# Issuing every second load of expert weights from ScalarE's queue instead of SyncE's

## The chip, the cores and the metric

The kernel runs on one core of a Trainium2 chip. A core has a matrix engine (TensorE, in the profile PE and PEld for its weight loads), VectorE (DVE), ScalarE (ACT), GpSimd (POOL) and SyncE (SP), each with one instruction stream that it works off in order, and DMA engines that move data between the chip's memory (HBM) and the core's own (SBUF). A transfer is issued by an instruction in the stream of some engine; an issue waits in that stream until the buffer that it fills is free. The metric is device time in microseconds (us).

## The reference

One sequence of 256 tokens with 1024 features goes through three blocks. All values are float32.

- Block 0: normalisation, a mixer of two linear recurrences (a gated one and retention), and a feed-forward layer with squared ReLU of 4096 features.
- Block 1: the same with a gated matrix memory (mLSTM) as mixer.
- Block 2: normalisation with a learnt shift and scale, causal attention of 8 heads beside a gated convolution, and a mixture of experts.

The mixture of experts is the part that matters here. A router scores 4 groups of 8 experts for each token; the token takes the best group and the two best experts in it. Each expert is a small network, and its result is weighted by the router:

```
g_idx = argmax(g_logits)
e_val, e_loc = top_k(e_logits[g_idx], 2)
hid = silu(xb @ w1[e]) * (xb @ w3[e])      # 1024 -> 512
y   = hid @ w2[e]                          # 512 -> 1024
out[tok] += weight * y
```

With 32 experts, `w1`, `w3` and `w2` are 201 MB, and the kernel reads all of it, whatever the router says.

## The kernel before, in words

The kernel is one Python function that traces instructions; a scheduler then puts each engine's instructions into one stream. It goes by an estimate of when an instruction can start, and among those that are ready by the order in which they were traced; `keep_in_program_order` pins an instruction behind the one traced before it on its engine. The stream is fixed before the program runs.

Up to the router the work is dense products. A weight unit of 1 MB (128 partitions x 4 x 512 numbers) is loaded by `load_unit` (L91) into one of seven ring buffers (`ring`, RA = 7). ScalarE copies each 128x512 tile of it to a rounded `wh` (L99), VectorE subtracts to get the rest `wl` (L100), and TensorE multiplies three times (`mm`, L106). Eight `wh` and eight `wl` buffers stand between them.

The experts follow. Their weights are 192 units of 1 MB in the order of `order` (L995): eight sets of four experts, each with 16 units in which `w1e` and `w3e` alternate (k even and odd), then eight of `w2e`. A unit goes into one of 20 places that the program names by its number k:

- units 0 to 7 in two halves each (`load_half`, L1008) in the general blocks (`b4`), 18 also there and 19 in a kept block (`k4`),
- units 8 to 14 in the seven ring buffers, 15 to 17 in three more (`ring2`), which take the memory of `wh` and `wl` once the last dense product is over,
- every later unit in the place of the one 18 before it. So a period has 8 units in halves (two issues each) and 10 whole.

`load_exp` (L1018) chooses the place and issues the load, from SyncE always. `ahead` (L1003) calls it early: for unit 19 and units 0 to 7 between the dense products of block 2, for 8 to 14 after the last one's loads, then for 15 to 18. From unit 20 on it is called where the unit is used, by `nxt` (L1208), and the scheduler may put it earlier, as far as its place is free.

One set of experts (`moe_pass`, L1179) is: `gather` (L1195) picks at most 32 tokens for each of four experts by a product with a one-hot matrix, four times for a quarter of the features, into `xg`, half of it written by VectorE (L1203) and half by ScalarE (L1204). Then 16 units are multiplied into `h1` and `h3`; ScalarE takes Silu of `h1` into `hid` (L1236), VectorE multiplies by `h3` (L1237), TensorE transposes. Then eight units of `w2e` are multiplied into `ye`, VectorE scales to `ys` (L1255), and `eacc` adds it to the tokens. ScalarE has five such instructions in a set: four `xg` and one `hid`. Experts with more than 32 tokens would be finished in further rounds (L1268); there are none with these inputs.

Of the kernel before, what the change touches and what calls it, by code (L numbers as in the profile page):

```python
# [19 lines left out]
P = 128  # L20
# [16 lines left out]
def kernel(ctx: ExitStack, tc: tile.TileContext, a, out, dbg=None):  # L37
# [35 lines left out]
    def tick(n=1, rep=1):  # L73
        """one more step (or rep) of each of the first n pieces of work beside the products"""
        for _ in range(rep):
            step(n)
# [32 lines left out]
    def dense_a(src, units, xh, xl, name, ticks=1):  # L109
        """512 output features on partitions: two tiles [128, 2, 256]; xh, xl: lists of [128, 4, 256]."""  # L110
        pp = [psm(name + "0", (P, 2, 256)), psm(name + "1", (P, 2, 256))]
        n = len(units)
        for kb, u in enumerate(units):
            raw = load_unit(src, u)
            for k in range(4):
                wh, wl = split(raw, k)
                first, last = kb == 0 and k == 0, kb == n - 1 and k == 3
                for ft in range(4):
                    o, w = pp[ft // 2][:, ft % 2, :], wh[:, ft * P:(ft + 1) * P]
                    mm(o, w, xh[kb][:, k, :], first and ft % 2 == 0, False)  # L120
                    mm(o, w, xl[kb][:, k, :], False, False)
                for ft in range(4):
                    mm(pp[ft // 2][:, ft % 2, :], wl[:, ft * P:(ft + 1) * P], xh[kb][:, k, :], False, last)
                if k % 2 == 1:
                    tick(ticks)
        return pp
# [6 lines left out]
    def dense_b(src, units, xh, xl, name=None, outs=None, first=True, last=True, ticks=1, rep=1):  # L133
        """tokens on partitions: outs[tt] [128, 512]."""
        if outs is None:
# [15 lines left out]
    def dense_first(src, units, xh, xl, name, between, raws=None, ws=()):  # L151
        """512 columns, tokens on partitions; the second tile of tokens, ready after between(), goes last"""
        outs = [psm(name + "0"), psm(name + "1")]
# [13 lines left out]
    def dense_out(src, kbs, yh, yl, acc, first, last, loaded=None, done=None):  # L167
        """rows kbs of a matrix of 1024 columns; the last rows go one half of the tokens after the other"""
        def out(tt, nb):
# [25 lines left out]
    def rsqrt_mean(ss, n, d, name):  # L195
        """(ss / d + eps) ** -0.5"""
        v = small(name + "v", n)
# [5 lines left out]
    def rms_halves(pieces, keep=False):  # L203
        """pieces: two APs [128, 512] of one row of 1024; the squares on ScalarE"""
        s = small("ss", 4)
# [30 lines left out]
    def trans_split(y, nk, tt, th, tl, kt0=0):  # L236
        """y [128 tok, nk*128] natural -> th/tl[kt // 4][:, kt % 4, tt*128:]"""
        for q in range(nk // 4):
# [6 lines left out]
    def norm_g(x, gB, name, shiftB=None):  # L245
        """rmsnorm(x) * gB (+ shiftB) for x [128, 1024]"""
        xg = b4("xg")
# [10 lines left out]
    def resid(acc, x, gB, tt):  # L258
        """x + rmsnorm(acc) * gB"""
        pieces = halves(acc)  # L260
# [9 lines left out]
    def gap(acc, x, gpost, gpre, name, fill, first, shiftB=None):  # L270
        """residual of a layer, norm of the next, its transpose and its first product"""
        th, tl = xt_tiles(2, name)
# [57 lines left out]
    def norm_gate(o, nh, dv, name, extra=None):  # L330
        """o [128, nh*dv] in psum -> o * rsqrt(mean(o*o)) per head; extra: a factor of o per head"""
        sq = b4(name + "sq", (P, nh * dv))
# [16 lines left out]

    # ------------------------------------------------------------------ loads of the start  # L350
    W = a["ev_w_in"]
# [14 lines left out]

    # ------------------------------------------------------------------ layer 0: hgrn2 and retention
    xh, xl = xt_tiles(2, "x0")
# [22 lines left out]
    xs.append(scaled(1))  # L391
    # values
    pv = dense_first(W, [4, 5], xh, xl, "pv", lambda: list(start(1)), raws, ws)
    vv = b4("hv", (P, 2, 512))
    for tt in range(2):
        S.activation(vv[:, tt, :], pv[tt], AF.Copy)
    # f
    pf = dense_a(W, [0, 1], xh, xl, "pf")
# [5 lines left out]
    at = 0  # L404
# [19 lines left out]

    # lower bound: softmax over the first axis, its first row
    e3 = b2.tile([P, 3, 4], F32, name="e3")
# [29 lines left out]
    bg.append(forget_bg())  # L456
    # q
    pq = dense_a(W, [2, 3], xh, xl, "pq")
# [12 lines left out]
    def hgrn_bg():  # L471
# [10 lines left out]
        for lev in range(7):  # L482
# [23 lines left out]
            if lev == 6:  # L506
                m6 = m
        # between the two tiles
        kl = b4("hkl", (P, 4, P))
# [16 lines left out]
        yield  # L526
        # out
        for tt in range(2):
# [19 lines left out]

    # retention
    def rope(pp):  # L550
# [48 lines left out]
    def gated(src, gate, func, g, nb, kt0):  # L599
        """src[tt][:, half nb] times the gate, transposed"""  # L600
        h = slice(nb * 512, nb * 512 + 512)
# [29 lines left out]
    dense_out(a["ev_w_out"], [2], yh, yl, acc, False, True)  # L631
    # ------------------------------------------------------------------ adaptive modulation
    scl = b2.tile([P, 8, 32], F32, name="scl")
# [60 lines left out]
    acc = mlp(a["w1_0"], a["w2_0"], xh, xl, o, mid(3))  # L694
    # gate weights, hi and lo, in columns 0..3 and 32..35 of 128
    wg = pk["wgate"].rearrange("p (k g)->p k g", k=8)
# [14 lines left out]

    # ------------------------------------------------------------------ layer 1: mlstm
    W = a["od_w_in"]
    gb15 = b2.tile([4, 2], F32, name="gb15")
    tc.keep_in_program_order(V.tensor_scalar_mul(gb15, pk["gate_b"][0:4, :], 1.0 / 15.0))

    # gates: rows [4 heads, 256 tokens]
    pg = psm("pg", (P, 512))
# [15 lines left out]
    def wd_bg():  # L734
# [8 lines left out]
        yield  # L743
        # columns: a_s and exp(-m_t)
        pc = psm("pc", (P, 4, 2, 4))
# [100 lines left out]

    # ------------------------------------------------------------------ attention and gated convolution
    cs8 = pk["cs8"].rearrange("p (a t i)->p a t i", a=2, t=2)
# [46 lines left out]
    def attn_bg():  # L895
# [3 lines left out]
        for tt, hh in ((0, (0, 8)), (1, (0, 4)), (1, (4, 8))):  # L899
# [4 lines left out]
            def pos(h):  # L904
                # even heads in one bank, odd heads in the other
                return (h % 2) * (nh // 2) + (h - hh[0]) // 2
# [47 lines left out]
    def rtile(name, shape):  # L954
        """a piece of one block for the small tiles of the routing"""
        n = int(np.prod(shape))
# [50 lines left out]

    def load_half(src, u, pin, alloc=b4):  # L1008
        t = []
        for i in range(2):  # L1010
            r = alloc("rawh", (P, 2, 512))
            d = nc.sync.dma_start(r, a[src][u][:, 2 * i:2 * i + 2, :])
            if pin:
                tc.keep_in_program_order(d)
            t.append(r)
        return lambda j: t[j // 2][:, j % 2, :]

    def load_exp(k, both, pin=False):  # L1018
        src, u = order[k]
        if both and k in once:  # L1020
            return load_half(src, u, pin, once[k])
        k = (k - 2 * (k > 1 + period)) % period
        if both and k < NBU:
            return load_half(src, u, pin)
        if both and k >= NBU + RA:
            r = ring2[0].tile([P, 4, 512], F32, tag="w2", name="raw2")
        else:
            r = ring.tile([P, 4, 512], F32, tag="w", name="raw")
        nc.sync.dma_start(r, a[src][u])
        return lambda j: r[:, j, :]  # L1030
# [28 lines left out]

    # ------------------------------------------------------------------ last product and routing  # L1060
    iota = pk["iota"]
# [48 lines left out]
    def first_max(v, m, n, name):  # L1110
        """one-hot of the first largest of v [P, m, n], and the largest"""
        mx = rtile(name + "m", [m])
# [8 lines left out]

    # the two largest of every group, and the group
    oh1, m1 = first_max(lge, 8, 8, "e1")
# [9 lines left out]
    V.tensor_mul(asg.rearrange("p t (g e)->p (t g) e", g=4), o12, gb)  # L1133
    # place of a token among its expert's tokens, from 1; 0 where it isn't the expert's
    pp = psm("pos", (P, 3, 32))
# [4 lines left out]
    V.scalar_tensor_tensor(place, pp[:, 0:2, :], 1.0, asg, ALU.add, ALU.mult)  # L1140
    # weights: softmax over the groups at the group, softmax over the two
    ge = rtile("ge", [2, 4])
# [36 lines left out]
    def moe_pass(acc, early):  # L1179
# [3 lines left out]
        def slots(g, factor):  # L1183
            """one-hot of the places of the experts of a group, times a factor"""
            sl = gpl.tile([P, 8, 32], F32, tag="sl", name="sl")
# [79 lines left out]
    moe_pass([pmm("eacc0"), pmm("eacc1")], early)  # L1265
    # tokens beyond 32 of an expert, 32 more in each round
    rounds = nc.values_load(nri[0:1, 0:1], min_val=0, max_val=7)
# [12 lines left out]
def layout(inputs):  # L1280
# [14 lines left out]
    def rp(m):  # L1295
        # columns (pair, head, half, 64) -> (half, pair, head, 64)
        return m.reshape(1024, 2, 2, 2, 64).transpose(0, 3, 1, 2, 4).reshape(1024, 512)
# [35 lines left out]
    o["w2e"] = np.ascontiguousarray(w.transpose(0, 4, 2, 3, 1, 5)).reshape(64, P, 4, 512)  # L1333
    # constants of the shapes alone
    g["onesq"] = np.ones((P, P), f32)
# [46 lines left out]
```

## Time and profile before

| what | value |
|---|---|
| time, three runs | 1357.7, 1358.58, 1359.63 us; median 1358.58 |
| profiled execution: span from the first to the last instruction | 1356.7 us (the page gives its time only so) |
| TensorE, VectorE, ScalarE, GpSimd busy in the span | 90%, 48%, 39%, 4% |
| read from HBM | 375.04 MB, on one queue |
| chain that ended last | TensorE 57%, DMA 33% |
| mean granted TensorE clock | 0.966 of full |

A row of a timeline has the start and the length in us, the engine, the line, the operation, what it writes and reads, and in brackets the idle time of the engine before it and what ended that. SPq is SyncE's queue of DMA issues. `x8` counts instructions that were merged; a product of one unit appears as eight, of a half unit as four. Windows give each engine's busy time in a stretch, the granted clock, the share of the DMA engines and what they moved. Times are from the span's start.

### The profile page before, as it was taken

The page shows a single profiled execution, that of the slowest core. Times are in us where ns is not written, and L with a number is a line of the kernel's source. Part 1 is how long each engine was busy: PE and PEld are TensorE (multiplying, and loading weights), DVE is VectorE, ACT ScalarE, POOL GpSimd, SP SyncE. Part 2 cuts the span into 40 slices and gives each one's busy share as a digit, 9 for nine tenths or more (in the row PEclk, how much of TensorE's full clock was granted, in tenths as well). Part 3 has the DMA queues.
Part 4 walks back from the last instruction along what each step waited for, and adds up shares of the span by engine and source line. Part 5 has one row for each costly group of instructions (what it writes and reads, how often), then busy time and mean ns, then how long its engine had stood idle before and what let it go on. Part 6 is the DMA issues. An engine that isn't in the chain of part 4 may idle for free.

```text
span 1356.7 us, 19131 instructions
## 1 busy us (share of the span) xinstructions
PE 1226.8 (90%) x7365; PEld 854.0 (63%) x7365; DVE 655.8 (48%) x1195; ACT 531.2 (39%) x943; POOL 49.1 (4%) x52
## 2 busy tenths in 40 slices
PE   7999999999999999999999999989777787877775
PEld 6997868999869876898967999953212121212111
DVE  6896767565667767656566774632101010101001
ACT  6844645555547645555555676411000000000000
POOL 0000011000010001000001200000000000000000
PEclk9999999999999999999999999989999898899878
DMA  8643457655475528555556546779999999999996
GB/s 346 264 167 144 141 198 290 220 187 193 178 291 198 203 98 332 180 190 188 193 202 275 222 159 252 293 293 419 414 413 417 418 415 413 418 418 414 414 417 244
DMA packets 67657, 377.41 MB, mean 278 GB/s; under 512 B 7900, under 2 KB 8924, under 8 KB 34280
## 3 DMA queue, kind: packets, MB, share of 16 engines
q1 hardware_dynamic: 67560, 376.12, 71.7%
q8 instruction: 60, 0.98, 0.3%
q14 instruction: 37, 0.30, 0.1%
HBM read 375.04 MB, written 1.05 MB: 277 GB/s over the span
## 4 chain that ended last, share of the span: by engine, by line
PE 57%; DMA 33%; DVE 4%; ACT 3%; issue 2%; POOL 1%; SPq 0%; ACTq 0%; DVEq 0%; POOLq 0%
PE acc L107 14%; PE h L107 13%; DMA raw<-in_w1e 9%; DMA rawh<-in_w2e 7%; DMA rawh<-in_w1e 6%; DMA rawh<-in_w3e 5%; DMA raw<-in_w2e 3%; PE pgt L107 3%; PE first L107 2%; PE pqk L107 2%; PE pog L107 2%; PE pqkv L107 2%; PE prg L107 1%; PE prv L107 1%; ACT wh L99 1%
## 5 line engine op out<-in xcount | busy, mean ns | idle before, releaser
L100 DVE TENSOR_TENSOR wl<-raw,wh 128x512 fp32r<-128x512 f32 x536 | 366.0, 698 | 211.7 <-ACT wh L99 208.4
L99 ACT ACTIVATE wh<-raw 128x512 fp32r<-128x512 f32 x536 | 332.0, 629 | 284.9 <-PE h L107 78.3
L107 PE MATMUL h<-raw,xg 128*32 128x512 f32 x560 | 88.2, 727 | 38.4 <-DMA raw<-in_w3e 19.5
L107 PE MATMUL h<-rawh,xg 128*32 128x512 f32 x464 | 99.7, 634 | 12.5 <-DMA rawh<-in_w3e 6.5
L1204 ACT ACTIVATE xg<-xgp,mcol 128x128 f32<-128x128 f32 x32 | 14.6, 457 | 240.5 <-DVE xg L1203 240.5
L107 PE MATMUL acc<-wh,hh 128*128 128x512 f32 x256 | 100.3, 392 | 0.5 <-ACT hh L225 0.5
L107 PE MATMUL acc<-wh,hl 128*128 128x512 f32 x256 | 99.8, 390 | 0.0
L107 PE MATMUL acc<-wl,hh 128*128 128x512 f32 x256 | 99.7, 389 | 0.0
L1237 DVE TENSOR_TENSOR hid<-hid,h 128x512 f32<-128x512 f32 x8 | 5.5, 687 | 175.8 <-PE h L107 146.1
L107 PEld LDWEIGHTS h<-raw,xg 128*32 128x32 f32 x560 | 13.7, 117 | 102.6 <-DMA raw<-in_w3e 44.2
L1236 ACT ACTIVATE hid<-h 128x512 f32<-128x512 f32 x8 | 4.8, 597 | 167.6 <-PE h L107 167.5
L107 PEld LDWEIGHTS h<-rawh,xg 128*32 128x32 f32 x464 | 16.8, 113 | 83.7 <-DMA rawh<-in_w3e 36.1
L1203 DVE TENSOR_SCALAR xg<-xgp,mcol 128x128 f32<-128x128 f32 x32 | 13.1, 410 | 109.2 <-PE xgp L107 109.2
L107 PE MATMUL ye<-raw,hT 128*32 128x512 f32 x256 | 39.0, 704 | 23.1 <-DMA raw<-in_w2e 19.1
L1255 DVE TENSOR_TENSOR ys<-ye,modB 128x512 f32<-128x512 f32 (+1 forms) x17 | 11.1, 660 | 97.8 <-PE ye L107 97.8
L107 PE MATMUL h<-x3h,wh 128*128 128x256 f32 x224 | 56.2, 284 | 0.0
L107 PE MATMUL h<-x1l,wh 128*128 128x256 f32 x224 | 56.2, 283 | 0.0
L107 PE MATMUL h<-x3l,wh 128*128 128x256 f32 x224 | 56.2, 283 | 0.0
L107 PE MATMUL h<-x1h,wh 128*128 128x256 f32 x224 | 56.1, 283 | 0.0
L107 PEld LDWEIGHTS acc<-wh,hh 128*128 128x128 f32 x256 | 48.1, 188 | 11.2 <-ACT hh L225 1.6
L107 PEld LDWEIGHTS acc<-wl,hh 128*128 128x128 f32 x256 | 48.1, 188 | 10.0
L107 PE MATMUL ye<-rawh,hT 128*32 128x512 f32 x256 | 47.8, 605 | 7.2 <-DMA rawh<-in_w2e 4.8
(502 smaller groups left out, 2469.6 us busy)
## 6 DMA issues: line engine op xcount, KB each, us to landing
raw<-in_w SPq DMA_DIRECT2D x64, 1024.0 KB, 4.8
raw<-in_w1e SPq DMA_DIRECT2D x35, 1024.0 KB, 16.2
raw<-in_w3e SPq DMA_DIRECT2D x35, 1024.0 KB, 17.4
rawh<-in_w2e SPq DMA_DIRECT2D x64, 512.0 KB, 11.2
raw<-in_w2e SPq DMA_DIRECT2D x32, 1024.0 KB, 16.1
rawh<-in_w1e SPq DMA_DIRECT2D x58, 512.0 KB, 10.2
rawh<-in_w3e SPq DMA_DIRECT2D x58, 512.0 KB, 10.2
raw<-in_w_ada SPq DMA_DIRECT2D x24, 1024.0 KB, 4.8
```

The costliest lines, as they stand in the source:

```text
L99: i = S.activation(wh, raw[:, k, :], AF.Copy)
L100: j = V.tensor_sub(wl, raw[:, k, :], wh.bitcast(F32))
L107: T.matmul(o, l, r, start=start, stop=stop, skip_group_check=True)
L1203: V.tensor_scalar(xg[:, k0, :], p[:, 0, :], sc2[:, k0:k0 + 1], sh2[:, k0:k0 + 1], ALU.mult, ALU.add)
L1204: S.activation(xg[:, k1, :], p[:, 1, :], AF.Identity, bias=sh2[:, k1:k1 + 1], scale=sc2[:, k1:k1 + 1])
L1236: S.activation(hid, h1, AF.Silu)
L1237: V.tensor_mul(hid, hid, h3)
L1255: V.tensor_mul(ys[:, c], y[:, c0:c0 + n], modB[5][:, c])
```

## The change

`load_exp` chooses the issuing queue by the unit's number: even ones stay on SyncE, odd ones go to ScalarE. That holds for the first pass only (`both`); further rounds stay on SyncE. Places, sizes and the order of the units are the same. `load_half` gets the queue as an argument, and its pin (used for unit 18) acts on the queue's engine. All other edits of the diff take out comments.

```
-    def load_half(src, u, pin, alloc=b4):
+    def load_half(src, u, pin, alloc, q):
         t = []
         for i in range(2):
             r = alloc("rawh", (P, 2, 512))
-            d = nc.sync.dma_start(r, a[src][u][:, 2 * i:2 * i + 2, :])
+            d = q.dma_start(r, a[src][u][:, 2 * i:2 * i + 2, :])
             if pin:
                 tc.keep_in_program_order(d)
             t.append(r)
...
     def load_exp(k, both, pin=False):
         src, u = order[k]
+        q = (nc.sync, nc.scalar)[k % 2 if both else 0]
         if both and k in once:
-            return load_half(src, u, pin, once[k])
+            return load_half(src, u, pin, once[k], q)
         k = (k - 2 * (k > 1 + period)) % period
         if both and k < NBU:
-            return load_half(src, u, pin)
+            return load_half(src, u, pin, b4, q)
...
-        nc.sync.dma_start(r, a[src][u])
+        q.dma_start(r, a[src][u])
         return lambda j: r[:, j, :]
```

So all units of `w3e` and every second one of `w2e` are issued by ScalarE, the rest by SyncE.

## Rows read from the trace of the kernel before

**Rows 1.** The page: what DMA moved in 40 equal slices of 33.9 us.

```profile
GB/s 346 264 167 144 141 198 290 220 187 193 178 291 198 203 98 332 180 190 188 193 202 275 222 159 252 293 293 419 414 413 417 418 415 413 418 418 414 414 417 244
```

**Rows 2.** Windows: engines' busy us (instructions), clock, DMA share, GB/s; the expert stage.

```profile
920.00:1342.00 422.00, 324.86 (x1744) 84.63 (x1736) 49.28 (x130) 18.24 (x37) 0.00 (x0) 0.91 1.02 415
```

**Rows 3.** The chain of waits, in order of time: start, us, what.

```profile
900.81 5.57 PE h L107 x32
...
918.99 11.38 DMA raw<-in_w1e
...
930.44 20.03 DMA raw<-in_w1e
...
1004.70 10.15 DMA rawh<-in_w1e
...
1329.86 12.52 DMA raw<-in_w2e
```

**Rows 4.** Timeline of SyncE's queue: the eighth issue from 918.99 on.

```profile
927.95 0.33 SPq L1029 DMA_DIRECT2D raw<-in_w3e  x1
```

**Rows 5.** DMA issues: what, queue, count, KB each, median us from issue to landing.

```profile
raw<-in_w SPq DMA_DIRECT2D x64, 1024.0 KB, 4.8
raw<-in_w1e SPq DMA_DIRECT2D x35, 1024.0 KB, 16.2
raw<-in_w3e SPq DMA_DIRECT2D x35, 1024.0 KB, 17.4
rawh<-in_w2e SPq DMA_DIRECT2D x64, 512.0 KB, 11.2
raw<-in_w2e SPq DMA_DIRECT2D x32, 1024.0 KB, 16.1
rawh<-in_w1e SPq DMA_DIRECT2D x58, 512.0 KB, 10.2
rawh<-in_w3e SPq DMA_DIRECT2D x58, 512.0 KB, 10.2
```

**Rows 6.** Timeline of SyncE's queue: unit 15, and the first half of unit 20.

```profile
888.06 0.33 SPq L1029 DMA_DIRECT2D raw<-in_w3e  x1
...
902.78 0.33 SPq L1012 DMA_DIRECT2D rawh<-in_w2e  x1
```

**Rows 7.** Windows: the dense part's end, and the first expert products.

```profile
850.00:890.00 40.00, 40.00 (x251) 35.87 (x250) 27.20 (x46) 17.29 (x32) 0.55 (x1) 1.00 0.74 272
...
900.00:904.00 4.00, 3.50 (x18) 0.81 (x21) 0.41 (x1) 0.46 (x1) 0.00 (x0) 0.50 0.10 33
```

**Rows 8.** Timeline of ScalarE: one of the splits in the dense part.

```profile
836.36 0.63 ACT L99 ACTIVATE wh<-raw 128x512 fp32r<-128x512 f32 x1 [0.81 <-PE pgt L107]
```

**Rows 9.** SyncE's waits in 860 to 890: us in total, times, longest.

```profile
SPq L1012 <- PE ppb L107: 2.5, 1, 2.5
```

**Rows 10.** Timeline of ScalarE: two instructions of the routing's chain.

```profile
888.00 0.63 ACT L1091 ACTIVATE junk<-xnew 128x512 bf16<-128x512 f32 x1 [0.40 <-DVE xnew L1088]
...
889.79 0.60 ACT L1076 ACTIVATE x5T<-tp 128x512 f32<-128x512 f32 x1 [0.58 <-PE tp L1075]
```

**Rows 11.** Waits between engines in 905 to 1342: us in total, times, longest.

```profile
ACT xg L1204 <- DVE xg L1203: 231.3, 31, 18.9
ACT hid L1236 <- PE h L107: 167.5, 7, 27.7
```

**Rows 12.** Timelines at the end of the stage: SyncE's queue, ScalarE and TensorE.

```profile
1309.59 18.03 SPq L1012 DMA_DIRECT2D rawh<-in_w2e  x12
...
1321.47 0.60 ACT L1236 ACTIVATE hid<-h 128x512 f32<-128x512 f32 x1 [27.68 <-PE h L107]
...
1325.50 1.06 PE L107 MATMUL ye<-rawh,hT 128*32 128x512 f32 x8 [0.78 <-DVE hT L1242]
...
1339.95 1.06 PE L107 MATMUL ye<-raw,hT 128*32 128x512 f32 x8 [1.41 <-DMA raw<-in_w2e]
...
1342.43 1.93 PE L107 MATMUL ye<-raw,hT 128*32 128x512 f32 x8 [1.41 <-DMA raw<-in_w2e]
```

More of the change, by code (lines that the diff above doesn't have):

```diff
@@ L1005, in ahead, with load_half @@
             early[k] = load_exp(k, True, pin)
-    def load_half(src, u, pin, alloc=b4):
+    def load_half(src, u, pin, alloc, q):
         t = []
@@ L1011, in load_half @@
             r = alloc("rawh", (P, 2, 512))
-            d = nc.sync.dma_start(r, a[src][u][:, 2 * i:2 * i + 2, :])
+            d = q.dma_start(r, a[src][u][:, 2 * i:2 * i + 2, :])
             if pin:
@@ L1019, in load_exp @@
         src, u = order[k]
+        q = (nc.sync, nc.scalar)[k % 2 if both else 0]
         if both and k in once:
-            return load_half(src, u, pin, once[k])
+            return load_half(src, u, pin, once[k], q)
         k = (k - 2 * (k > 1 + period)) % period
         if both and k < NBU:
-            return load_half(src, u, pin)
+            return load_half(src, u, pin, b4, q)
         if both and k >= NBU + RA:
@@ L1028, in load_exp @@
             r = ring.tile([P, 4, 512], F32, tag="w", name="raw")
-        nc.sync.dma_start(r, a[src][u])
+        q.dma_start(r, a[src][u])
         return lambda j: r[:, j, :]
```

## Prediction, before the result was known

> **What bounds the kernel now.** I read the page's forty slices first [rows 1]: from the 28th on, about 915 us, DMA moves 413 to 419 GB/s in every slice but the last; up to there it is 98 to 346. So there are two programs: the dense one, and the expert stage, which reads weights. The stage's own windows say it harder [rows 2]: in 920 to 1342 us the DMA share is 1.02 at 415 GB/s, and ScalarE works 18.24 of 422 us. The chain of waits [rows 3] is one load after another, joined by SyncE's queue, and the queue's issues [rows 4] show why: the load issued at 918.99 is followed by seven more up to 927.95, and the ninth, at 930.44, starts when the first has landed (11.38 us). Eight loads are in flight, always. Eight whole units issued from 930.44 take 20.03 us, 2.504 us for each MB unit; eight half units take 10.15 us, 1.270 us each. Units 20 to 191 are what is left when the stage starts; by the counts of issues [rows 5] (102 whole, 180 half), less the first twenty units (10 whole, 20 half by the code), these are 92 whole and 160 half loads: 92 x 2.504 + 160 x 1.270 = 433.6 us. From the first of them, issued at 902.78 [rows 6], to the last landing at 1342.38 (1329.86 + 12.52, rows 3) it is 439.6 us. The stage is its transfers, with 6 us of start.
>
> The sum is made against the profiled span of 1356.7 us; the runs' median of 1358.58 lies 1.9 us above it, outside of the first and last instruction, and nothing in the change touches that.
>
> **Part 1: the rate.** Eight whole units in flight are 8 MB, eight halves 4 MB, and both saturate the engines [rows 2, 3]; so the amount in flight is not the limit, and neither is issuing: one issue takes SyncE 0.33 us [rows 4], an eighth of the 2.504 us of a unit. Taking half of the issues off SyncE buys nothing there. What two queues do to the rate no row shows, since all loads of before are on one. Bounds: a whole unit costs 2 x 1.270 - 2.504 = 0.036 us less than its two halves; that is what the seam between two loads costs. If a second queue hid every seam, 252 x 0.036 = 9.1 us would go; if two streams cost one more seam for each load, 9.1 us would come. I take 0, since the share is already over 1.
>
> The row is the share of 1.02 with one queue [rows 2]. The Trainium skill (DMA: Bandwidth & Descriptors, "Issuing engines are not separate DMA queues") says that loads issued by different engines end on the same sixteen DMA engines and interleave, and that only the issuing time is saved. By that rule this term is 0 and neither of its ends is reached; no run here shows it yet.
>
> **Part 2: the dense part, up to 888 us.** ScalarE gets units 1, 3, 5, 7, 19 (ten half loads) and 9, 11, 13: 13 issues x 0.33 = 4.3 us. This lies beside TensorE, which is busy 40.00 of 40 us up to 890 [rows 7]. ScalarE's splits there wait for TensorE each time: 0.81 us of idle and 0.63 of work, a period of 1.44 [rows 8], because all eight `wh` buffers are full; it is up to eight tiles, 11.5 us, ahead. An issue of 0.33 us fits into one gap. Some loads must wait for a buffer, and now ScalarE stands there with its splits behind it; such waits of SyncE are 2.5 us for halves [rows 9], and a ring buffer is freed by VectorE's subtraction right behind the split. Both are inside 11.5 us: 0. Without that cover it would be 4.3 us + four waits of 2.5, some 14 us.
>
> **Part 3: the routing.** Units 15 and 17 wait for the buffers of the last dense product, and SyncE issues the first of them at 888.06 [rows 6], in the middle of the serial chain Square, transpose, logits on ScalarE [rows 10]. Two issues are 0.66 us; ScalarE's idle time in this stretch is 0.40 + 0.58 us. So it is 0 if they fall into gaps and 0.66 if not; I take 0.3. A delay here counts in full: TensorE's first expert products at 900.81 [rows 3] free the buffers for unit 20 onward, and DMA stands at a share of 0.10 in 900 to 904 [rows 7].
>
> **Part 4: the stage itself.** 126 of the 252 loads are ScalarE's: 126 x 0.33 = 42 us beside 18 us of work in 422. The issue is not the cost, the place in the stream is. ScalarE stood 231.3 us before its 31 `xg` and 167.5 us before seven `hid` [rows 11]: these waits end when TensorE has a unit that is just landing. A load that stands behind such a wait can't be issued earlier. How the stream mixes the two no row of before shows. From both sides: with the loads a few units ahead of the work, nothing, since at every stop one or two whole loads (2.5 to 5 us) are still on their way, and SyncE's half goes on; it may run 18 units ahead, which is what the buffers hold. With ScalarE dry at each stop, a lone load takes 4.8 us from issue to landing [rows 5] against 2.5 in the stream: 2.3 us exposed; three stops a group (`hid`, the first `xg`, the other three) in seven groups make 48 us. I take 0, because to leave the engines idle both queues have to be dry at once. Odd loads will be late and even ones early, which TensorE can take: it needs 1.06 us for a unit [rows 12].
>
> **Part 5: the end.** In before unit 190 lands first, its product runs at 1339.95 (1.06 us), and unit 191's at 1342.43 [rows 12]. If both land together, or the odd ones last with the even one waiting behind a late 189, one more product stands behind the last landing: 0 to 2 units, 0 to 2.1 us. I take one, 1.1 us.
>
> How two queues share the engines no run here shows. The Trainium skill (DMA: Bandwidth & Descriptors, "Queues, rings and completion order") says that each DMA engine takes packets in turn from the queues that have work, so that neighbours progress side by side. By it the two last units land together, and this term is 1.1.
>
> **Sum.** 0 + 0 + 0.3 + 0 + 1.1 = +1.4 us: a span of 1358.1 and a time of 1360.0 us. By the pages' two rules it is the same.
>
> **Rivals.**
> A, slower: ScalarE's loads stand behind its own waits. The place is `hid`, its longest stop (27.7 us, rows 11). It decides from the point where fewer than one whole unit is in flight on ScalarE's queue and SyncE's has run into its 18 buffers. For it: 400 us of waiting on that engine, all on products that need loads. Against: SyncE refills whenever TensorE frees a buffer. Price: once a group, 7 x 2.3 = 16 us: 1376; partly so, anything between.
> B, faster: the second queue hides the seams: -9.1 + 1.4: 1350.9. For it: the 0.036 us between halves and wholes. Against: a share of 1.02.
> C, slower: the reverse order. The loads stand far ahead in ScalarE's stream, wait for a landing, and hold `xg` and `hid` behind them. DMA hides it in the middle; at the end there are no more loads. If the last group's `xg` wait until unit 187 is issued, about 1321 (eighth of the twelve issues in 18.03 us from 1309.59, rows 12), some 14 products (15 us), `hid` to `ye` (1321.47 to 1325.50, 4 us), eight products (8.5 us) and the sums between (2.7 us) end at 1351 instead of 1344.4 (1342.43 + 1.93): +7, with the 1.4 of the sum 1367.
> D, slower: two streams disturb each other by 1%: 433.6 x 0.01 = 4.3 us, with the 1.4: 1364.
> That the change does not do what it says can be seen by ScalarE's issue rows alone; the code leaves the later rounds on SyncE, and in before nothing of them runs.
>
> **Chances.** Forecast 0.53, its own range 1357 to 1361.5; A 0.18, B 0.12, C 0.12, D 0.05. Some 0.2% (2.7 us) is what can be told from no change. B gives faster 0.11, with 0.02 of the forecast: 0.13. A, C, D less what stays small give 0.30, with 0.02 of the forecast: 0.32. Same is 0.55. The range 1354.5 to 1371 holds the forecast, C, D, half of B and a third of A, 0.82; A in full and B in full are left out.
>
> **What would show it.** Right: SyncE's loads of rows 5 halve and as many stand on ScalarE's queue; share 1.02 and 415 GB/s again in the stage; first expert product within 0.5 us of 900.8; the last two units landing together. Part 1 wrong: a rate off 415 by over 1% with the share still full. Part 4 wrong: a share under 0.98 in some stretches, with TensorE waiting for odd units and ScalarE at `hid` before them. Part 5 wrong: more than two products behind the last landing. Parts 2 and 3 wrong: the first expert product later than 902.

## The result, and the profile after

The changed kernel takes 1367.88 us (1365.98 to 1369.54, four runs) against 1358.16 (1357.70 to 1359.63, four runs): 1.0067 times as long, 95% interval 1.0054 to 1.0080. That is slower, inside the stated range, and 7.9 us above the forecast; the likeliest case, no change, did not come. The profiled span is 1367.8 us, 11.1 more than before. Those 11.1 us fall into four parts, each read from rows below:

| stretch | before | after | difference |
|---|---|---|---|
| up to the first expert product | 900.81 | 904.51 | +3.7 |
| from there to the last landing | 441.58 | 445.97 | +4.4 |
| from the last landing to the end of the last VectorE sum | 6.74 | 9.16 | +2.4 |
| from there to the end of the span | 7.53 | 8.13 | +0.6 |

The change does what it says. The DMA issues of the changed kernel, columns as in [rows 5]:

```profile
raw<-in_w3e ACTq DMA_DIRECT2D x35, 1024.0 KB, 13.4
rawh<-in_w3e ACTq DMA_DIRECT2D x58, 512.0 KB, 11.4
rawh<-in_w2e ACTq DMA_DIRECT2D x32, 512.0 KB, 12.6
raw<-in_w2e ACTq DMA_DIRECT2D x16, 1024.0 KB, 12.9
```

All w3e loads and half of the w2e loads stand on ScalarE's queue; from issue to landing a whole unit takes some 13 us (16 to 17 in [rows 5]), a half unit 11 to 13 (10 to 11).

**The first part** is one stop of TensorE, in the dense part, at 738 us. The chain of waits of the changed kernel there, then its first expert product and its last piece:

```profile
738.53 1.69 POOL qr L200
740.22 0.02 issue
740.25 0.69 DVE nat L867
740.94 0.08 DVE mcol L672
741.02 0.04 issue
741.06 10.50 PE pqkv L107 x45
...
904.51 4.59 PE h L107 x32
...
1359.22 0.42 DVE xnew L1262
```

TensorE's next `pqkv` needs the accumulator that VectorE's `mcol` (L672) reads last, and `mcol` stands behind `nat` (L867), which waits for GpSimd's `qr`. VectorE's timeline of the kernel before has the two the other way round:

```profile
731.58 0.16 DVE L672 SCALAR_TENSOR_TENSOR mcol<-mcol,packg 128x4 f32<-128x4 f32 x1 [0.57 <-PE mcol L667]
738.21 0.69 DVE L867 TENSOR_TENSOR nat<-nat,qr 128x512 f32<-128x512 f32 x1 [6.47 <-POOL qr L200]
```

There `mcol` was done over six microseconds before GpSimd was, and TensorE never stopped. Neither line is touched by the change. The stop is 2.8 of the 3.7 us; the other 0.9 lie in the first load of the program (landed at 9.68 instead of 8.74 us), ahead of anything that differs.

**The second part.** Windows of the changed kernel, columns as in [rows 2]; the first is just behind that stop, the others are in the expert stage:

```profile
740.50:744.00 3.50, 2.94 (x13) 2.45 (x14) 3.50 (x13) 1.27 (x2) 0.00 (x0) 1.00 0.26 40
...
1040.00:1080.00 40.00, 32.03 (x173) 10.41 (x174) 3.99 (x7) 1.37 (x3) 0.00 (x0) 0.84 1.02 416
1080.00:1120.00 40.00, 30.27 (x167) 9.15 (x165) 5.61 (x15) 1.51 (x3) 0.00 (x0) 0.95 0.99 397
1120.00:1160.00 40.00, 28.91 (x172) 10.27 (x170) 4.55 (x14) 1.97 (x4) 0.00 (x0) 0.86 1.00 402
1160.00:1200.00 40.00, 29.91 (x160) 9.25 (x158) 2.61 (x5) 1.37 (x3) 0.00 (x0) 0.80 1.02 409
...
920.00:1342.00 422.00, 317.88 (x1728) 97.70 (x1728) 48.92 (x137) 20.90 (x41) 0.00 (x0) 0.83 1.02 411
```

Most of the stage runs at 416 GB/s, as before: where the share is 1.02, two streams cost no rate. From 1080 to 1200 us it is 397 to 409; (416 - 402.7) x 120 us / 416 makes 3.8 us. What SyncE waited for, in 1070 to 1200 us (first row) and in the whole stage (second row):

```profile
SPq L1030 <- PE h L107: 21.7, 3, 10.4
...
SPq L1012 <- DMA rawh<-in_w3e: 56.0, 18, 5.8
```

The first is new: SyncE stood 10.4 us at a stretch before buffers that TensorE had not freed; before, all its waits for products in this window were under 1 us. The second is a wait for a landing of ScalarE's. The program gives the loads of both engines the same eight semaphores to report their landing on, and a load waits until the one before it on its semaphore has landed; so the eight loads in flight are counted over both queues, and a late load of ScalarE's holds SyncE as well. ScalarE's own waits in 905 to 1350 us, columns as in [rows 11]:

```profile
ACT xg L1205 <- DVE xg L1204: 198.5, 20, 27.9
ACT hid L1237 <- PE h L107: 62.3, 5, 21.6
ACT xg L1205 <- DMA rawh<-in_w3e: 51.2, 4, 23.6
```

With the smaller groups they add up to 413 us, about as much as the 399 of [rows 11], but loads now stand behind them. It goes the other way too: 13 of these waits, 146 us, ended with the landing of a load, since `xg` or `hid` stood behind a load that waited.

**The third part**, the end. ScalarE's and SyncE's queues and TensorE in the changed kernel's timelines, to be held against [rows 12]:

```profile
1329.70 0.60 ACT L1237 ACTIVATE hid<-h 128x512 f32<-128x512 f32 x1 [9.30 <-DMA rawh<-in_w3e]
1329.71 0.82 ACTq L1012 DMA_DIRECT2D rawh<-in_w2e  x2
1330.86 0.33 ACTq L1030 DMA_DIRECT2D raw<-in_w2e  x1
1334.19 6.88 ACTq L1012 DMA_DIRECT2D rawh<-in_w2e  x4
...
1313.90 0.33 SPq L1030 DMA_DIRECT2D raw<-in_w2e  x1
1323.00 14.92 SPq L1012 DMA_DIRECT2D rawh<-in_w2e  x6
...
1346.61 3.48 PE L107 MATMUL ye<-rawh,hT 128*32 128x512 f32 x10 [4.06 <-DMA rawh<-in_w2e]
1350.76 1.98 PE L107 MATMUL eacc<-ys,swT 128*128 128x512 f32 x4 [0.67 <-DVE ys L1256]
1352.67 1.49 PE L107 MATMUL ye<-rawh,hT 128*32 128x512 f32 x11
```

The last group's whole w2e units are 190 and 191, the last that TensorE needs. SyncE issues 190 at 1313.90, 9 us ahead of the halves of 184; ScalarE issues 191 at 1330.86, ahead of 187 and 189. TensorE waits 4.06 us for a half of 187 and then has five units still to multiply. The last half, of 189, lands 9.9 us behind its issue at 1340.6 (the last of the four from 1334.19 on), at 1350.5, and almost four units are left then:

```profile
rawh<-in_w2e ACTq DMA_DIRECT2D x2, 512.0 KB, 9.9
```

In before, 8 rows of products stood behind the last landing [rows 12]; here it is 30, with the sums between them (one unit is 8 in this count). The end of before's chain, for the table above:

```profile
1344.91 3.77 PE eacc L107 x8
...
1348.71 0.42 DVE xnew L1261
```

The order of the loads in the two built programs, by unit (xg and hid are ScalarE's own instructions between them), shows that this isn't confined to the end:

```
before   SyncE    172 173 174 175 176 177 178 179 180 181 182 183 184 185 186 187 188 189 190 191
changed  SyncE    172 166 174 168 170 176 182 178 180 190 184 186 188
changed  ScalarE  173 167 xg 169 175 171 xg xg 177 179 xg 181 183 hid 185 191 187 189
```

With one issuing engine the planner kept the loads in unit order. With two it set whole units (172 to 181, 190, 191) ahead of half units that TensorE needs first. So "the order of the units is the same" holds for the order in which the loads are traced, not for the one in which the program issues them.

### The profile page after: what moved, and what is told of

It reads as the page before. It is cut to its first block, busy times and chain, and to the rows that moved or that the text cites. A ratio compares the mean times of both kernels' runs of the same rounds, so it can differ in the third digit from the quotient of the medians.

```text
span 1367.8 us, 18966 instructions
## 1 busy us (share of the span) xinstructions
PE 1222.6 (89%) x7365; PEld 867.4 (63%) x7365; DVE 654.7 (48%) x1195; ACT 530.9 (39%) x943; POOL 50.2 (4%) x52
## 4 chain that ended last, share of the span: by engine, by line
PE 59%; DMA 29%; DVE 5%; ACT 3%; issue 2%; POOL 1%; SPq 0%; ACTq 0%; POOLq 0%; DVEq 0%
PE h L107 14%; PE acc L107 14%; DMA rawh<-in_w2e 8%; DMA rawh<-in_w1e 7%; DMA rawh<-in_w3e 5%; DMA raw<-in_w1e 3%; PE pgt L107 3%; DMA raw<-in_w2e 3%; PE first L107 2%; PE pqk L107 2%; DMA raw<-in_w3e 2%; PE pog L107 2%; PE prg L107 1%; PE prv L107 1%; DVE wl L100 1%
## 5 line engine op out<-in xcount | busy, mean ns | idle before, releaser
L107 PE MATMUL h<-rawh,xg 128*32 128x512 f32 x464 | 109.5, 747 | 43.8 <-DMA rawh<-in_w3e 31.0
L1205 ACT ACTIVATE xg<-xgp,mcol 128x128 f32<-128x128 f32 x32 | 14.6, 457 | 335.1 <-DVE xg L1204 198.5
L107 PE MATMUL h<-raw,xg 128*32 128x512 f32 x560 | 81.1, 636 | 16.1 <-ACT xg L1205 6.1
L107 PE MATMUL ye<-rawh,hT 128*32 128x512 f32 x256 | 55.7, 701 | 26.5 <-DMA rawh<-in_w2e 24.1
L1256 DVE TENSOR_TENSOR ys<-ye,modB 128x512 f32<-128x512 f32 (+1 forms) x17 | 11.1, 658 | 125.1 <-PE ye L107 125.1
L107 PEld LDWEIGHTS h<-raw,xg 128*32 128x32 f32 x560 | 21.8, 114 | 56.3 <-issue 32.0
L107 PEld LDWEIGHTS xgp<-sl,xnew 128*128 128x128 f32 x256 | 33.9, 205 | 34.6 <-issue 30.6
L107 PEld LDWEIGHTS acc<-wh,hh 128*128 128x128 f32 x256 | 48.1, 188 | 11.1 <-ACT hh L225 1.6
L107 PEld LDWEIGHTS acc<-wh,hl 128*128 128x128 f32 x256 | 48.1, 188 | 9.5
L107 PEld LDWEIGHTS ye<-rawh,hT 128*32 128x32 f32 x256 | 10.1, 120 | 65.8 <-DMA rawh<-in_w2e 39.1
```

What stands on the lines that cost most here:

```text
L107: T.matmul(o, l, r, start=start, stop=stop, skip_group_check=True)
L1205: S.activation(xg[:, k1, :], p[:, 1, :], AF.Identity, bias=sh2[:, k1:k1 + 1], scale=sc2[:, k1:k1 + 1])
L1256: V.tensor_mul(ys[:, c], y[:, c0:c0 + n], modB[5][:, c])
```

## Experiments

Each ratio is to the kernel before, run beside it on the same chip. Theory S in the first expectations: the stop at 738 us, and for the stage and the end ScalarE's own waits in front of its loads.

**1. Unit 19 back on SyncE.**

```
-        q = (nc.sync, nc.scalar)[k % 2 if both else 0]
+        q = (nc.sync, nc.scalar)[k % 2 if both and k != 19 else 0]
```

> Only unit 19 goes back to SyncE; every other odd unit stays on ScalarE. Theory S (three places): of the 11.1 us that the changed kernel's profiled span is longer, 2.8 are one stop of TensorE at 738 us, because moving unit 19's two half loads to ScalarE made the planner set VectorE's L867 (which waits for GpSimd) ahead of L672 (which frees TensorE's next accumulator). Then the stop is gone and the time is 1367.9 - 2.8 = 1365.1 us. Rival R (two streams disturb each other everywhere): the dense part's delay is the loads' and stays: 1367.9 us.

Measured: 1362.48 us (1362.09 to 1363.01), 1.0031 [1.0018, 1.0043]. TensorE is busy throughout the window of the stop:

```profile
736.00:740.50 4.50, 4.50 (x22) 3.72 (x21) 1.71 (x6) 3.19 (x6) 1.69 (x1) 1.00 0.01 4
```

The built program differs from the changed kernel in unit 19's two issues and in the order of VectorE's and ScalarE's instructions around L672 and L867; every other load stands where it stood, and L672 is first again. So the stop is shown, and where it comes from. But the time fell by 5.4 us, twice what was expected: in the profile 3.1 us up to the first product (901.45), the rest in the stage and the end, whose loads have the same order. Experiment 4 accounts for a part of it.

**2. The last group on SyncE.**

```
+        q = (nc.sync, nc.scalar)[k % 2 if both and k < 168 else 0]
```

> The last group's 24 units (168 to 191) go back to SyncE, all earlier odd units stay on ScalarE. Theory S: the end of the changed kernel lost 2.4 us behind the last landing (9.2 against 6.8 us) and some 1.5 to 2 us while the queues ran dry from 1330 us on, both because ScalarE's last loads stood behind its own wait for hid; these go: 1363.5 to 1364.5 us, last landing to end of the last VectorE add 6.8 us. Rival R: the loss is spread over the stage and the last group holds 1/8 of it: 1367 us.

Measured: 1364.33 us, 1.0044 [1.0031, 1.0058], so 3.6 us less than the changed kernel: the end is a part of its own, as S has it.

**3. Only the last group on two engines.**

```
+        q = (nc.sync, nc.scalar)[k % 2 if both and k >= 168 else 0]
```

> The complement: only the last group's odd units are on ScalarE, all others on SyncE. Theory S: before plus the 2.4 us behind the last landing plus up to 2 us of dry queues: 1360.6 to 1362.6 us. Rival R: 1/8 of the loss, 1358.2 + 0.7 = 1358.9 us.

Measured: 1361.79 us, 1.0025 [1.0014, 1.0035]: 24 of 192 units bring 3.7 of the 9.7 us.

**4. Only the early units on two engines.**

```
+        q = (nc.sync, nc.scalar)[k % 2 if both and k < 20 else 0]
```

> Only odd units below 20 (loaded in the dense part) are on ScalarE; from unit 20 on SyncE issues all. Theory S: before plus the one stop of TensorE at 738 us: 1358.2 + 2.8 = 1361.0 us, and the stage as before (share 1.02, 415 GB/s). Rival R: two streams cost nothing where DMA is not full: 1358.2 us. The prediction's own bound for this part, ScalarE's splits pushed back, would show as idle TensorE at other places up to 890 us: up to 1372 us.

Measured: 1362.44 us, 1.0029 [1.0020, 1.0038], and the stage runs at 416 GB/s. The stop itself is there, and it costs more than in the changed kernel's profile. The window behind it, and the first expert product by the chain:

```profile
740.50:744.00 3.50, 3.00 (x9) 2.36 (x10) 3.50 (x13) 0.63 (x1) 0.00 (x0) 0.68 0.30 47
```

```profile
906.03 4.23 PE h L107 x21
```

The granted clock is 0.68 here, between the levels of 1.2 and 2.4 GHz, and was 1.00 in the changed kernel; the same products took that much longer, and the first expert product came 5.2 us later than in [rows 3], 0.9 of it from the first load. A stop of 2.4 us (the idle time) cost 2.8 us in the changed kernel's profile, and one of 2.2 us 4.3 here.

**5. GpSimd in ScalarE's place.**

```
+        q = (nc.sync, nc.gpsimd)[k % 2 if both and k != 19 else 0]
```

> As the kernel with only unit 19 on SyncE (1362.5 us, 4.4 above before), but the odd units are issued by GpSimd, which has no other work in the stage and so no waits of its own in front of a load. Theory S (what is left of the loss is ScalarE's loads behind its waits for xg and hid, in the stage and at the end): two issuing engines stay, the loss goes: 1358 to 1359.5 us, no stretch of 40 us under 413 GB/s. Rival R (two issuing engines land out of TensorE's order, whoever issues): 1362 us again.

Measured: 1365.06 us, 1.0047 [1.0032, 1.0061]. S falls as it was put: an engine with no other work in the stage loses as much. Again 30 rows of products stand behind the last landing, and a window of the stage lacks rate:

```profile
1080.00:1120.00 40.00, 25.85 (x142) 7.23 (x140) 2.48 (x4) 1.05 (x2) 6.82 (x13) 0.80 0.97 386
```

The built program has 191 ahead of 183, and 190 ahead of 182. So the order of the loads became a theory of its own (P in experiments 9 to 11).

**6. ScalarE's part of xg on VectorE.** (Unit 19 on SyncE.)

```
-            S.activation(xg[:, k1, :], p[:, 1, :], AF.Identity, bias=..., scale=...)
+            V.tensor_scalar(xg[:, k1, :], p[:, 1, :], sc2[...], sh2[...], ALU.mult, ALU.add)
```

> Unit 19 on SyncE, other odd units on ScalarE, and ScalarE's half of each xg goes to VectorE: ScalarE keeps only the eight hid and its waits for xg (some 320 us in the stage) are gone. Theory S: half or more of the 4.4 us go, 1359 to 1361 us; what stays is the end, where the last w2 loads stand behind hid. Rival R: 1362.5 us, or 0.4 us more for each gather that TensorE waits for.

Measured: 1363.22 us, 1.0031 [1.0018, 1.0043], the same ratio as in experiment 1. Taking away the waits for xg brings nothing; in this order of loads they were not the cost. (190 and 191 stand ahead of half units here too, and 30 rows behind the last landing.)

**7. All loads on ScalarE.**

```
+        q = (nc.sync, nc.scalar)[1 if both and k != 19 else 0]
```

> All expert loads but unit 19 are on ScalarE: one queue, in TensorE's order, every load behind ScalarE's own waits, and no SyncE that goes on meanwhile. Theory S: at each stop the engines run dry; by the prediction's bounds 2.3 us at three stops in seven groups, up to 48 us, at least the 16 of one stop a group: 1374 to 1406 us, with a DMA share clearly below 1.02. Rival R (only two queues lose): one queue again, 1358 to 1360 us.

Measured: 1412.42 us, 1.0407 [1.0391, 1.0423].

```profile
920.00:1342.00 422.00, 316.76 (x1586) 79.02 (x1578) 46.27 (x127) 17.73 (x35) 0.00 (x0) 0.88 0.94 371
```

One queue, and 371 GB/s instead of 415 [rows 2]. So the waits do hold loads, by some 50 us, when no other engine issues meanwhile.

**8. Only the middle of the stage on two engines.**

```
+        q = (nc.sync, nc.scalar)[k % 2 if both and 20 <= k < 168 else 0]
```

> Odd units from 20 to 167 are on ScalarE, the early ones and the last group on SyncE: only the middle of the stage is changed. Theory S: before plus the stage's own part, which in the kernel with unit 19 on SyncE was some 1 to 2 us (405 to 406 GB/s from 1080 to 1160 us): 1359 to 1360.5 us; with the early part (+4.4) and the last group alone (+3.7) it should then sum to the changed kernel's 9.7. Rival R (all of the stage's loss arises at the end): 1358.2 us.

Measured: 1360.37 us (1357.76 to 1363.58), 1.0012 [1.0003, 1.0021]. The three parts sum to 4.4 + 3.7 + 1.7 = 9.8 us; the whole change is 9.7. The middle's own part varies from run to run by more than its size.

**9. Unit order kept, with ScalarE.** (Unit 19 on SyncE here and in the next two.)

```
         src, u = order[k]
+        pin = pin or k >= 20
 ...
+        d = q.dma_start(r, a[src][u])
+        if pin:
+            tc.keep_in_program_order(d)
```

> As the kernel with only unit 19 on SyncE (1362.5 us), but every load from unit 20 on is kept in the program's order on its engine; with two issuing engines the planner had put whole units ahead of half units that TensorE needs first (190 ahead of 184 on SyncE, 191 ahead of 187 and 189 on ScalarE). Theory P (the loss is this order): TensorE's products behind the last landing fall from 30 rows to 8 to 16, the stage from first product to last landing is 441.6 us again: 1358.5 to 1360 us. Rival S (ScalarE's loads behind its waits for xg and hid): the waits are still in front of the loads: 1362.5 us or up to 16 us more. Rival R (two issuers as such): 1362.5 us.

Measured: 1392.62 us, 1.0251 [1.0237, 1.0265]. Behind the last landing only 8 rows of products stand, as P has it; but the stage takes 31 us more, as S has it. A window near the stage's start, and what SyncE waited for in the stage:

```profile
920.00:940.00 20.00, 17.12 (x102) 5.77 (x98) 6.24 (x21) 2.02 (x3) 0.00 (x0) 0.91 0.46 161
```

```profile
SPq L1012 <- DMA raw<-in_w3e: 117.5, 18, 11.7
SPq L1031 <- DMA rawh<-in_w3e: 109.4, 25, 13.5
```

w3e is all ScalarE's. SyncE, which does nothing but issue, waits for landings of ScalarE's loads, and those are issued behind xg and hid.

But the edit changes more than the order of the units. The pin puts a load behind the instruction traced before it, and on ScalarE that is an `xg` or the `hid` next to its use. The first `w3e` unit of the second group of experts (25), in the changed kernel and then here:

```profile
913.73 0.33 ACTq L1012 DMA_DIRECT2D rawh<-in_w3e  x1
```

```profile
938.62 0.46 ACT L1208 ACTIVATE xg<-xgp,mcol 128x128 f32<-128x128 f32 x1 [17.04 <-DVE xg L1207]
938.64 1.78 ACTq L1012 DMA_DIRECT2D rawh<-in_w3e  x4
```

In the changed kernel its first half is issued among the `xg` of the group before; here it stands behind the first `xg` of its own group, which it is multiplied with. The 31 us are what ScalarE's waits cost when its loads have no lead. What unit order with the lead kept would cost no run shows, so this is no test of P in the stage.

**10. Unit order kept, with GpSimd.** The edit of experiment 9, with nc.gpsimd.

> The same order of units with GpSimd in ScalarE's place (out of order it took 1365.1 us): two issuing engines, no waits of GpSimd's own, loads in TensorE's order. Theories P and S both expect 1358 to 1359.5 us; rival R (two issuers land out of order anyway) 1365 us. If this is fast and the run with ScalarE in unit order is not, ScalarE's waits are what is left.

Measured: 1358.18 us (1357.26 to 1359.03), 0.9995 [0.9986, 1.0004].

```profile
1080.00:1120.00 40.00, 30.49 (x162) 10.48 (x162) 3.58 (x6) 1.51 (x3) 6.33 (x12) 0.87 1.02 415
...
920.00:1342.00 422.00, 314.74 (x1733) 95.20 (x1732) 48.61 (x127) 17.51 (x36) 60.67 (x115) 0.91 1.02 414
```

Two issuing engines, no `xg` and `hid` in front of the loads, loads in unit order: from the first expert product to the last landing it is 441.7 us, against 441.6 in before. R falls, and with experiment 5 beside it the order alone is worth 0.52% with GpSimd. Against experiment 9 three things differ at once: GpSimd has no waits of other work, the pin takes no lead from it, and its loads report on eight semaphores of their own, so SyncE no longer waits for them. Which of the three saves the 31 us these runs don't part.

**11. Only the last eight units in order, with ScalarE.** `pin = pin or k >= 184`.

> As the kernel with only unit 19 on SyncE, but only the last eight units (184 to 191) are kept in order; nothing else of the stage moves. Theory P: the end's part alone goes: rows of products behind the last landing 8 to 16 instead of 30, the tail 6 to 7 us instead of 8.1, and the time 1360.5 to 1361.5 us. Rivals S and R: hid is still ahead of ScalarE's last loads, and two issuers stay: 1362.5 us, tail 8 us.

Measured: 1359.00 us, 1.0005 [0.9996, 1.0014]; experiment 1 stood at 1.0031. TensorE's timeline at the end:

```profile
1342.92 2.30 PE L107 MATMUL ye<-rawh,hT 128*32 128x512 f32 x14
1345.85 1.92 PE L107 MATMUL ye<-raw,hT 128*32 128x512 f32 x16 [0.63 <-DMA raw<-in_w2e]
1348.33 2.34 PE L107 MATMUL eacc<-ys,swT 128*128 128x256 f32 x8 [0.55 <-DVE ys L1259]
```

TensorE now waits for the whole units, the last of its order, and 8 rows stand behind the last landing. The loads up to 183 stand as in experiment 1, so P is right for the end, and the gain was over its 1 to 2 us: in the profiles the time from the last landing to the last VectorE sum falls from 8.1 us to 4.5. Before takes 6.7 us for the same 8 rows, at a lower granted clock (experiment 12).

**12. TensorE kept busy at the end of before.** All loads are SyncE's again.

```
                         mm(y[e, :], hT[:, fc, e], raw(j), fc == 0, fc == 3)
+                    if w2 and nb and fc in (1, 2):
+                        again = psm("again")
+                        for j in range(4):
+                            e = slice(32 * j, 32 * j + 32)
+                            mm(again[e, :], hT[:, fc, e], raw(j), True, True)
```

> Before itself (all loads on SyncE) with eight products more: those of units 189 and 190, the last but two and the last but one, are done a second time into a tile that nothing reads. They fill the 1.41 us in which TensorE waits for units 190 and 191. Reason: behind the last landing before took 6.74 us at a granted clock of 0.5, three kernels of this study took 4.46 to 4.54 us for the same instructions at 1.00. Theory: if TensorE's clock stays up because it is busy, the last product takes 1.06 instead of 1.93 us, the sums 2.34 instead of 3.76, the tail is 4.5 us and the time 1356.7 us (1358.9 - 2.2). Rival: the clock falls all the same, the products done twice then take 1.93 us and push the last one back by up to 1.4 us: 1359 to 1360.3 us.

Measured: 1357.45 us (1355.84 to 1357.78), 0.9988 [0.9979, 0.9997]: faster than both kernels. TensorE's timeline:

```profile
1340.27 1.06 PE L107 MATMUL ye<-raw,hT 128*32 128x512 f32 x8 [0.57 <-DMA raw<-in_w2e]
1341.15 1.04 PE L107 MATMUL again<-raw,hT 128*32 128x512 f32 x8
1342.75 1.06 PE L107 MATMUL ye<-raw,hT 128*32 128x512 f32 x8 [0.56 <-DMA raw<-in_w2e]
1344.37 2.34 PE L107 MATMUL eacc<-ys,swT 128*128 128x256 f32 x8 [0.55 <-DVE ys L1260]
```

The windows behind the last landing, this kernel's and then before's, show the granted clock:

```profile
1342.00:1348.00 6.00, 3.52 (x20) 1.43 (x16) 2.44 (x6) 0.00 (x0) 0.00 (x0) 1.00 0.30 104
```

```profile
1342.00:1349.00 7.00, 5.69 (x16) 2.37 (x16) 2.32 (x6) 0.00 (x0) 0.00 (x0) 0.54 0.17 61
```

The last product takes 1.06 us instead of 1.93 [rows 12], the sums 2.34 instead of 3.77. Expected were 2.2 us, measured are 1.5.

## Why the prediction was right and wrong

The time lies inside the stated range, but not in the forecast's own, 1357 to 1361.5 us. The stated range holds it because it leaves room for rivals C and D and a part of A, and no run shows one of them as the cause: that it held is luck.

**Part 1, the rate: right.** 416 GB/s with two streams against 415 [rows 2], where the share is full, and in experiment 10 the whole stage takes 441.7 us against 441.6. Rival B (seams hidden) and rival D (streams disturb each other) fall with it. The Trainium skill (DMA: Bandwidth & Descriptors, "Issuing engines are not separate DMA queues") says that only issuing time is saved; the 1.02 and 414 GB/s of experiment 10 agree.

**Part 2, the dense part: wrong, 0 instead of 2.8 to 4.3 us.** The step reckoned with ScalarE's issues and splits, and these did stay hidden: no other stop of TensorE appeared. It took the order of every other instruction for given. But the kernel's order is a planner's, and moving two issues to ScalarE turned round two VectorE instructions that no load touches. Nothing in the profile of before could price that; that it could happen was to be seen from the fact that a planner writes the order, and it should have widened the term.

**Part 3, the routing: within its bounds.** From the first routing transpose to the first expert product it is 904.51 - 889.89 = 14.6 us, in before 900.81 - 886.20 = 14.6. The issue falls into a gap.

**Part 4, the stage: wrong, 0 instead of 4.4 us in the profile (1.7 us by experiment 8 for its middle).** The step that failed is "to leave the engines idle both queues have to be dry at once". They are not independent: SyncE's loads wait for landings of ScalarE's, and for buffers that TensorE frees only in unit order. The other half was that it left the order of the loads open ("how the stream mixes the two no row of before shows") and then took it to be in unit order. What the runs show in its place: with GpSimd the order is all of the loss (experiments 5 and 10), and with ScalarE it is the loss at the end (experiment 11). For the middle of the stage with ScalarE the order is argued, not shown: experiment 6 takes the waits for xg away and gains nothing, and experiment 9 changes more than the order. ScalarE's waits cost 31 us where its loads have no lead (experiment 9), and some 50 where no other engine issues (experiment 7).

**Part 5, the end: mis-sized, 1.1 instead of 2.4 us.** "0 to 2 units" behind the last landing were almost four, since the last landing is not the last unit. The 2.4 us even understate it: the 30 rows ran at a granted clock of 1.00 and before's 8 at 0.54, and against 8 rows at 1.00 (4.5 us, experiments 2, 10 and 11) they cost 4.7 us. The Trainium skill (DMA: Bandwidth & Descriptors, "Queues, rings and completion order") lets neighbours progress side by side, and in experiment 11, where two engines issue 190 and 191 last, these land 0.8 us apart (1345.81 and 1346.59), which agrees; it was not that which set this term, since 8 rows stand behind them as in before.

**The rivals.** C gave 1367, within a microsecond of the measured time, by a mechanism that isn't there where C priced it: the last group's four xg ran from 1294 to 1320 us, and unit 187 was issued behind them and behind hid, from 1334.19 on. In the stage xg and hid did stand behind waiting loads (146 us), which C took to be hidden. "Right" by C's number would have been luck. A is the mechanism of experiments 7 and 9, with some 50 and 31 us where the prediction priced it at 16; in the changed kernel no run shows a cost of it.

**Open.** Experiment 1 gained 5.4 us, of which its stop explains 2.8 to 4.3. The stage's own part differs by up to 3 us between profiles of kernels with the same order of loads (1.2 us over before in experiment 1, 4.4 in the changed kernel, 3.8 in experiment 11), and the eleven runs of experiment 8 reach from 1357.76 to 1363.58 us; which small delay decides this was not found.

## What to carry to other kernels

Where a planner writes the order, moving a DMA's issue is a change of order on every engine: compare the order of the built programs, not only the queues. Two issuing engines over one saturated set of transfers gain nothing, and where the planner takes loads out of the order of use, transfers stay full while the wrong data lands; keep them in that order. On an engine with other work that is not done by a pin alone: here the pin also put each load behind the work next to its use, and took its lead. A load behind an engine's own waits also holds the loads of the other engine, where both report on the same semaphores.

## What the runs showed of the hardware

- More in flight brought no rate: GpSimd's loads have eight semaphores of their own in the program, and in experiment 10 twelve to sixteen loads were in flight instead of seven to eight. A whole w1e unit then took 24.9 us from issue to landing against 16.2 [rows 5], at 414 GB/s against 415. One of GpSimd's issues took 0.53 us, SyncE's 0.33.
- The same instructions behind the last landing took 6.7 us in before, at a granted clock of 0.54 (nearly the level of 1.2 GHz), and 4.5 us in experiments 2, 10 and 11. In before TensorE had been busy 1.61 of the 4 us up to 1342; in experiment 12, busy 3.43 of 4 us by doing eight products twice, it kept 1.00.
- Behind one stop of 2.2 to 2.4 us in a busy stretch the granted clock was 1.00 in one profile, 0.66 and 0.68 in two others (experiments 2 and 4): the stop's price differs by 1.5 us between the profiles of the changed kernel and of experiment 4.
